# Loading the next seven-product chunk ahead of plain weight loads in a one-core decoder layer

## The chip, the cores and the metric

The kernel runs on one core of a Trainium2 chip. The metric is the device time of one execution in microseconds (us). The core's engines are TensorE (PE: matmuls; PEld is its weight load), VectorE (DVE), ScalarE (ACT), GpSimd (POOL) and SyncE (SP); each works through its own list of instructions in order. SP issues nearly all weight loads from memory; POOL issues loads and stores that add to what is there.

## The reference

One layer on 256 tokens of width 2048, in float32: a half-step gated feed-forward network (FFN) and a layer norm, then a mixer of two branches (attention over keys that an indexer selects, and a gated linear recurrence) and a layer norm, then a second FFN and a layer norm.

```python
def swiglu(h, w_in, w_out):
    a, b = jnp.split(h @ w_in, 2, axis=-1)
    return (jax.nn.silu(a) * b) @ w_out
...
h = layer_norm(DN_ALPHA * h + 0.5 * swiglu(h, ffn1_w_in[l], ffn1_w_out[l]), ln1_g[l], ln1_b[l])
q, k, v, qi, ki, wi, rx, rg, gates = split_cols(h @ w_in[l])
...
merged = g_attn * (y_attn @ w_attn_branch[l]) + g_rnn * (y_rnn @ w_rnn_branch[l])
h = layer_norm(DN_ALPHA * h + merged @ w_out[l], ln2_g[l], ln2_b[l])
h = layer_norm(DN_ALPHA * h + 0.5 * swiglu(h, ffn2_w_in[l], ffn2_w_out[l]), ln3_g[l], ln3_b[l])
```

The FFN's inner width is 5632. All weights are read once, so the kernel streams them through on-chip buffers while TensorE multiplies.

## The kernel before

Each float32 product is made of three matmuls on operands that are split into a high part and a rest: `wh` (made by ACT, line 268) and `wl` (made by DVE, line 269) of a weight, `xh` and `xl` of an activation; lines 727 to 729 are the three. So every weight passes a load (SP), a copy on ACT and a subtraction on DVE before PE can use it.

The weights are a list of pieces. A plain piece has 128x1024 elements (512 KB) and lands in a tile `raw`, of which there are 4. A chunk has 128x2048 elements (1 MB) and lands in a tile `rf`; it stands for four pieces in a row (`p1q3`, `p2`, `q5p7`, `q4p6`), since it is multiplied by a scheme of seven products in place of eight. For that DVE makes sums of the chunk's quarters first: `ws` (line 228) and two sums back into `rf` (lines 232 and 235). `rf` has 2 buffers; in the two FFNs a third one (tag `r3`) takes every third chunk. Chunks take these buffers in turn, so a chunk's buffer is free once the last split of the chunk three before it (two before it, where there are two buffers) is done on DVE.

`Weights.unit` hands PE its weights one after the other. Each time a new piece begins (`cur`), it runs `far_to` (pieces of f1o and f2o that are marked far: loaded early, split on ACT alone into `wd` by lines 180 and 183, with the rest made by POOL's adding load, line 181), then `load_to`, which issues loads up to 8 pieces ahead of `cur` in the order of the list (line 214; line 173 for far ones), and `split_to`, which splits up to 4 ahead.

The order of the instructions on PE, SP and POOL is that of the program. On ACT and DVE a scheduler sets it when the kernel is built, from its own estimate of when each instruction's inputs are there; on the chip that order is fixed, and an instruction that waits holds up all behind it on its engine.

The FFN runs in 22 blocks of 256 inner columns, each with four column groups of the first weight matrix (f1a, f2a). Blocks 6 to 21 of each FFN take all four as chunks: a block is three plain pieces of the second matrix (f1o, f2o: the `o` fills of blocks before it), two chunks, one more plain piece, two chunks. Two of the four plain pieces of a block are mostly far ones. Their finished sums leave as `yd` (ACT, line 1154), which POOL adds to memory (`ya`, line 1155).

Of the kernel before, what the change touches and what calls it, by code (L numbers as in the profile page):

```python
# [8 lines left out]
F32 = mybir.dt.float32  # L9
# [6 lines left out]
P = 128  # L16
# [41 lines left out]
RAWF_BUFS = 2  # L58
# [2 lines left out]
AHEAD = 4  # L61
EARLY = 12
LOADS = 4
FORMS = ("p1q3", "p2", "q5p7", "q4p6")
PIECE = 1024
FAST = (0, 1, 2, 3)
# [4 lines left out]
def block_plan(chunks, fills, lead=2, n=4, late=True):  # L71
# [3 lines left out]
    plain = [("c", k) for q in range(n) if q not in chunks for k in (4 * q, 4 * q + 2)]  # L75
    forms = [(f, q) for q in chunks for f in FORMS]
    rest = ["o"] * fills
# [58 lines left out]
class Weights:  # L136
# [8 lines left out]
    def __init__(self, nc, pool, pieces, on_piece):  # L145
        self.nc, self.pool, self.on_piece = nc, pool, on_piece
        self.fast_pool = self.third = None
        self.chunks = 0
        self.wide = None
        self.pieces = pieces  # L150
        self.raw = {}
        self.sums = {}
        self.hl = {}
        self.loaded = 0
        self.split = 0
        self.cur = -1
        self.limit = None
        self.cap = len(pieces)
        self.off = 0
        self.far = []  # L160
        self.apart = ()
        self.far_raw = {}
        self.far_loaded = self.far_split = 0

    def far_to(self, i):


        nc = self.nc
        while self.far_loaded < len(self.far) and self.far[self.far_loaded] <= i + LOADS:
            k = self.far[self.far_loaded]  # L170
# [24 lines left out]
    def load_to(self, i, between=None):  # L195
        nc = self.nc
        while self.loaded <= min(i, len(self.pieces) - 1):
            ap, form = self.pieces[self.loaded]
            k = self.key(self.loaded)
            if k not in self.raw and self.loaded not in self.far:  # L200
                n = ap.shape[1]
                if form:
                    self.chunks += 1
                    if self.third and self.chunks % 3 == 0:
                        t = self.third.tile([P, 2 * PIECE], F32, name=f"rf{self.loaded}", tag="r3", bufs=1)
                    else:
                        t = self.fast_pool.tile([P, 2 * PIECE], F32, name=f"rf{self.loaded}", tag="rf", bufs=RAWF_BUFS)
                else:
                    t = self.pool.tile([P, PIECE], F32, name=f"raw{self.loaded}", tag="raw", bufs=RAW_BUFS)
                self.raw[k] = t  # L210
                if between:
                    between(self.loaded)
                if self.loaded:
                    nc.sync.dma_start(t[:, :n], ap)
                else:
                    nc.sync.dma_start(t[:, :n // 2], ap[:, :n // 2])
                    nc.sync.dma_start(t[:, n // 2:n], ap[:, n // 2:])
            self.loaded += 1

    def operand(self, k, form):  # L220


        v = self.nc.vector
        b = self.raw[k].rearrange("p (r j c) -> p j r c", r=2, j=4)
        if form == "p1q3":
            t = self.fast_pool.tile([P, PIECE], F32, name=f"ws{self.split}", tag="ws", bufs=WS_BUFS)
            t = self.sums[k] = t.rearrange("p (f r c) -> p f r c", f=2, r=2)
            v.tensor_tensor(t, b[:, 0:4:3], b[:, 1:2].to_broadcast([P, 2, 2, 256]), op=OP.add)  # L228
            return b[:, 0:4:3]
        t = self.sums[k]  # L230
        if form == "p2":
            v.tensor_tensor(b[:, 1], t[:, 1], b[:, 0], op=OP.add)  # L232
            return b[:, 2:3]
        if form == "q5p7":
            v.tensor_tensor(b[:, 0], b[:, 1], b[:, 2], op=OP.add)  # L235
            return t
        del self.sums[k]
        return b[:, 0:2]

    def split_to(self, i, step=PIECE):  # L240
        nc = self.nc
        while self.split <= min(i, len(self.pieces) - 1):
# [27 lines left out]
            self.hl[self.split] = (h, l)  # L270
            if form in (None, FORMS[-1]):
                del self.raw[k]
            self.split += 1

    def unit(self, n):
        if self.cur < 0 or self.off == self.size(self.cur):
            self.hl.pop(self.cur, None)
            self.cur += 1
            self.off = 0
            self.far_to(self.cur + EARLY)  # L280
            self.load_to(self.cur + AHEAD + LOADS)
            self.split_to(self.limit or min(self.cur + AHEAD, self.cap))
            self.on_piece()
        h, l = self.hl[self.cur]
        o = self.off
        self.off += n
        assert self.off <= self.size(self.cur)
        if self.cur in self.apart or self.cur in self.far:
            return h[o // 512], l[o // 512]
        return h[:, o:o + n], l[:, o:o + n]  # L290
# [1379 lines left out]
```

## Time and profile before

| | |
|---|---|
| time, median of 3 runs | 2363.15 us (2363.1 to 2363.26) |
| the profiled execution's own time | 2361.44 us |
| its span, first to last instruction | 2359.6 us |
| PE busy | 2343.0 us (99%) |
| DVE busy | 2202.7 us (93%) |
| ACT busy | 1564.7 us (66%) |
| chunk loads of the FFNs (f1a, f2a) | 75 and 75, 1 MB each |
| read from memory | 507.10 MB |

Busy times of different engines overlap. A matmul's end is modelled, so a PE that is busy all the time can still be held up a little by each operand; the starts of its matmuls tell. Idle time of DVE, ACT and SP costs only what reaches PE.

### The profile page before, as it was taken

What the parts mean: (1) busy time and instruction counts of PE and PEld (TensorE: products, weight loads), DVE (VectorE), ACT (ScalarE), POOL (GpSimd) and SP (SyncE); (2) the same over time, 40 slices, a digit from 0 to 9 for tenths busy, and PEclk for the clock granted to TensorE, in tenths of its full rate; (3) what the DMA queues carried; (4) which work ended last, traced back from release to release, by engine and by line L of the source; (5) the groups of instructions that cost most, each with busy time, mean ns of one, the idle gap of its engine ahead of it and who ended that gap; (6) DMA issues with size and microseconds to landing.
All of it is one profiled execution on the core that took longest, in us unless ns stands there. A gap on an engine that the chain in (4) does not pass through costs nothing.

```text
span 2359.6 us, 40531 instructions
## 1 busy us (share of the span) xinstructions
PE 2343.0 (99%) x15430; PEld 2120.5 (90%) x15430; DVE 2202.7 (93%) x3197; ACT 1564.7 (66%) x2271; POOL 269.4 (11%) x376
## 2 busy tenths in 40 slices
PE   9999999999999999999999999999999999999998
PEld 7899999999988999888899998888889999999997
DVE  7999999999999999879887778998999999999997
ACT  7677777777656656556557785555767777777763
POOL 1111111111110000000100001100111111111111
PEclk9999999999999999999999999999999999999999
DMA  9888898888866555554665658755788888888876
GB/s 333 251 240 242 248 267 243 254 247 258 245 209 228 191 188 200 181 185 143 246 237 187 201 175 305 257 192 175 240 271 238 254 253 247 242 263 258 247 224 209
DMA packets 141667, 546.98 MB, mean 232 GB/s; under 512 B 16640, under 2 KB 17280, under 8 KB 117024
## 3 DMA queue, kind: packets, MB, share of 16 engines
q1 hardware_dynamic: 99792, 453.03, 54.8%
q0 software_dynamic: 41680, 91.36, 18.8%
q8 instruction: 121, 1.98, 0.3%
q14 instruction: 74, 0.61, 0.1%
HBM read 507.10 MB, written 37.22 MB: 231 GB/s over the span
## 4 chain that ended last, share of the span: by engine, by line
PE 86%; DVE 7%; issue 3%; DMA 2%; ACT 1%; POOL 0%; SPq 0%; POOLq 0%; ACTq 0%; DVEq 0%
PE mm L727 18%; PE mm L728 18%; PE mm L729 18%; PE bp L728 7%; PE bp L729 7%; PE bp L727 7%; DVE wl L269 4%; PE mm L1363 3%; PE mm L1364 3%; PE mm L1365 3%; DVE ws L228 1%; PE bp L1131 1%; DVE rf L232 1%; DVE rf L235 0%; ACT wh L268 0%
## 5 line engine op out<-in xcount | busy, mean ns | idle before, releaser
L268 ACT ACTIVATE wh<-rf 128x1024 fp32r<-128x1024 f32 x573 | 512.3, 913 | 236.6 <-DVE rf L235 123.1
L269 DVE TENSOR_TENSOR wl<-rf,wh 128x1024 fp32r<-128x1024 f32 x573 | 592.8, 1040 | 11.6 <-ACT wh L268 7.8
L268 ACT ACTIVATE wh<-raw 128x1024 fp32r<-128x1024 f32 (+3 forms) x402 | 409.8, 1038 | 205.4 <-PE mm L729 99.8
L269 DVE TENSOR_TENSOR wl<-raw,wh 128x1024 fp32r<-128x1024 f32 (+3 forms) x402 | 472.9, 1193 | 71.6 <-ACT wh L268 69.7
L728 PE MATMUL bp<-wl,sh 128*128 128x256 f32 x1146 | 322.5, 281 | 0.8 <-DVE wl L269 0.8
L727 PE MATMUL bp<-wh,sh 128*128 128x256 f32 x1146 | 320.5, 280 | 0.0
L729 PE MATMUL bp<-wh,sl 128*128 128x256 f32 x1146 | 320.2, 279 | 0.0
L727 PE MATMUL mm<-wh,hs 128*128 128x512 f32 (+1 forms) x800 | 276.1, 345 | 0.8 <-DVE z L1119 0.5
L729 PE MATMUL mm<-wh,hs 128*128 128x512 f32 (+1 forms) x800 | 270.1, 338 | 1.3 <-DVE hs L863 1.3
L728 PE MATMUL mm<-wl,hs 128*128 128x512 f32 (+1 forms) x800 | 269.7, 337 | 0.0
L268 ACT ACTIVATE wh<-ws 128x1024 fp32r<-128x1024 f32 x191 | 202.1, 1058 | 92.5 <-DVE ws L228 58.3
L228 DVE TENSOR_TENSOR ws<-rf 128x1024 f32<-128x1024 f32 x191 | 232.7, 1218 | 11.4 <-DMA rf<-wA 3.1
L269 DVE TENSOR_TENSOR wl<-ws,wh 128x1024 fp32r<-128x1024 f32 x191 | 232.4, 1217 | 3.0 <-ACT wh L268 3.0
L728 PEld LDWEIGHTS bp<-wl,sh 128*128 128x128 f32 x1146 | 215.4, 188 | 5.3 <-DVE wl L269 1.6
L727 PEld LDWEIGHTS bp<-wh,sh 128*128 128x128 f32 x1146 | 215.4, 188 | 1.5
L729 PEld LDWEIGHTS bp<-wh,sl 128*128 128x128 f32 x1146 | 215.4, 188 | 0.0
L1363 PE MATMUL mm<-hs,wh 128*128 128x256 f32 x640 | 180.3, 282 | 0.0
L1364 PE MATMUL mm<-hs,wh 128*128 128x256 f32 x640 | 179.8, 281 | 0.0
L1365 PE MATMUL mm<-hs,wl 128*128 128x256 f32 x640 | 179.8, 281 | 0.0
L729 PEld LDWEIGHTS mm<-wh,hs 128*128 128x128 f32 x800 | 150.2, 188 | 20.7 <-DVE hs L863 2.1
L727 PEld LDWEIGHTS mm<-wh,hs 128*128 128x128 f32 x800 | 150.3, 188 | 19.4 <-issue 2.2
L728 PEld LDWEIGHTS mm<-wl,hs 128*128 128x128 f32 x800 | 150.4, 188 | 16.1
(358 smaller groups left out, 5903.4 us busy)
## 6 DMA issues: line engine op xcount, KB each, us to landing
rf<-f1a SPq DMA_DIRECT2D x75, 1024.0 KB, 7.8
rf<-f2a SPq DMA_DIRECT2D x75, 1024.0 KB, 7.7
raw<-f1o SPq DMA_DIRECT2D x88, 512.0 KB, 6.6
raw<-f2o SPq DMA_DIRECT2D x88, 512.0 KB, 6.7
raw<-wB SPq DMA_DIRECT2D x80, 512.0 KB, 4.8
raw<-wG SPq DMA_DIRECT2D x54, 512.0 KB, 4.4
ya<-yd POOLq DMA_DIRECT2D x80, 256.0 KB, 7.8
rf<-wA SPq DMA_DIRECT2D x20, 1024.0 KB, 5.1
```

Of the source, the lines that this page charges most:

```text
L228: v.tensor_tensor(t, b[:, 0:4:3], b[:, 1:2].to_broadcast([P, 2, 2, 256]), op=OP.add)
L232: v.tensor_tensor(b[:, 1], t[:, 1], b[:, 0], op=OP.add)
L268: nc.scalar.activation(hp, src, AF.Copy)
L269: self.last = nc.vector.tensor_tensor(lp, src, hp, op=OP.subtract)
L727: T.matmul(ps, xh, w[0], start=start, stop=False)
L728: T.matmul(ps, xh, w[1], start=False, stop=False)
L729: T.matmul(ps, xl, w[0], start=False, stop=stop)
L1131: T.transpose(ps[:, k * S + t * P:k * S + (t + 1) * P], z[:, t * 512 + k * P:t * 512 + (k + 1) * P], ident)
L1363: T.matmul(ps[:, :S], w[0], x[:, 0], start=first, stop=False)
L1364: T.matmul(ps[:, :S], w[0], x[:, 1], start=False, stop=False)
L1365: T.matmul(ps[:, :S], w[1], x[:, 0], start=False, stop=last)
```

## The change

A new method `load_chunk` runs after `load_to` at each new piece. It looks up to 4 pieces past the last one loaded for a chunk whose load has not been issued. If that chunk's turn is not the third buffer's, none has been loaded early already, and fewer than 2 chunks stand unsplit before it, the chunk's load is issued at once, in front of the plain loads between. `load_to` then passes over it. Buffers, sizes and computation stay as they are.

```diff
--- before.py
+++ after.py
@@ -61,6 +61,7 @@
 AHEAD = 4
 EARLY = 12
 LOADS = 4
+CHUNK_LOADS = 4
 FORMS = ("p1q3", "p2", "q5p7", "q4p6")
 PIECE = 1024
 FAST = (0, 1, 2, 3)
@@ -152,6 +153,7 @@
         self.sums = {}
         self.hl = {}
         self.loaded = 0
+        self.early = set()
         self.split = 0
         self.cur = -1
         self.limit = None
@@ -197,6 +199,7 @@
         while self.loaded <= min(i, len(self.pieces) - 1):
             ap, form = self.pieces[self.loaded]
             k = self.key(self.loaded)
+            self.early.discard(k)
             if k not in self.raw and self.loaded not in self.far:
                 n = ap.shape[1]
                 if form:
@@ -216,6 +219,25 @@
                     nc.sync.dma_start(t[:, :n // 2], ap[:, :n // 2])
                     nc.sync.dma_start(t[:, n // 2:n], ap[:, n // 2:])
             self.loaded += 1
+
+    def load_chunk(self, end):
+
+
+        for i in range(self.loaded, min(end, len(self.pieces))):
+            ap, form = self.pieces[i]
+            k = self.key(i)
+            if not form or k in self.raw or i in self.far:
+                continue
+            if self.third and (self.chunks + 1) % 3 == 0 or self.early:
+                return
+            busy = {self.key(j) for j in range(self.split, i) if self.pieces[j][1]}
+            if len(busy) >= RAWF_BUFS:
+                return
+            self.chunks += 1
+            self.early.add(k)
+            t = self.raw[k] = self.fast_pool.tile([P, 2 * PIECE], F32, name=f"rf{i}", tag="rf", bufs=RAWF_BUFS)
+            self.nc.sync.dma_start(t, ap)
+            return
 
     def operand(self, k, form):
 
@@ -279,6 +301,7 @@
             self.off = 0
             self.far_to(self.cur + EARLY)
             self.load_to(self.cur + AHEAD + LOADS)
+            self.load_chunk(self.loaded + CHUNK_LOADS)
             self.split_to(self.limit or min(self.cur + AHEAD, self.cap))
             self.on_piece()
         h, l = self.hl[self.cur]
```

PE's and POOL's lists keep their order. SP's, ACT's and DVE's change. In 10 blocks of the first FFN and 11 of the second the load of the next block's first chunk moves ahead of two plain loads, one of them far; in the blocks between, whose next chunk is the third buffer's, nothing moves on SP. Elsewhere 47 more chunk loads move ahead of 1 to 3 loads (one near the start, ahead of 9).

SP in the middle of the first FFN, before; the number after the name is the piece. Chunk 274 is a block's fourth; the next block begins with plain 278, far 279 and plain 280, then come its chunks 281 and 285 and its far piece 289:

```order
L214 DMA rf274_5329<-f1a 128x2048
L214 DMA raw278_5409<-f1o 128x1024
L214 DMA raw280_5440<-f1o 128x1024
L173 DMA raw289_5459<-f1o 128x1024
L214 DMA rf281_5461<-f1a 128x2048
L214 DMA rf285_5527<-f1a 128x2048
```

and with the change:

```order
L217 DMA rf274_5329<-f1a 128x2048
L217 DMA raw278_5409<-f1o 128x1024
L239 DMA rf281_5411<-f1a 128x2048
L217 DMA raw280_5442<-f1o 128x1024
L175 DMA raw289_5461<-f1o 128x1024
L239 DMA rf285_5479<-f1a 128x2048
```

The chunk 281 now stands before plain 280 and far 289, which come after it.

ACT in the same block, from the third split of the block's third chunk (272) to the fourth of its fourth (277), before:

```order
L268 ACTIVATE wh272_5370<-ws270_5333 128x1024
L180 ACTIVATE wd352_5519<-raw289_5459 128x512
L180 ACTIVATE wd353_5520<-raw289_5459 128x512
L183 ACTIVATE wd350_5517<-raw289_5459 128x512
L268 ACTIVATE wh273_5387<-rf270_5258 128x1024
L1154 ACTIVATE yd348_5403<-mm335_5184 128x512
L1154 ACTIVATE yd349_5406<-mm336_5185 128x512
L268 ACTIVATE wh274_5411<-rf274_5329 128x1024
L268 ACTIVATE wh275_5429<-rf274_5329 128x512
L268 ACTIVATE wh276_5442<-ws274_5413 128x1024
L183 ACTIVATE wd351_5518<-raw289_5459 128x512
L268 ACTIVATE wh277_5463<-rf274_5329 128x1024
```

and with the change:

```order
L290 ACTIVATE wh272_5370<-ws270_5333 128x1024
L290 ACTIVATE wh273_5387<-rf270_5240 128x1024
L1177 ACTIVATE yd348_5403<-mm335_5184 128x512
L1177 ACTIVATE yd349_5406<-mm336_5185 128x512
L290 ACTIVATE wh274_5413<-rf274_5329 128x1024
L290 ACTIVATE wh275_5431<-rf274_5329 128x512
L290 ACTIVATE wh276_5444<-ws274_5415 128x1024
L182 ACTIVATE wd352_5521<-raw289_5461 128x512
L182 ACTIVATE wd353_5522<-raw289_5461 128x512
L185 ACTIVATE wd350_5519<-raw289_5461 128x512
L185 ACTIVATE wd351_5520<-raw289_5461 128x512
L290 ACTIVATE wh277_5463<-rf274_5329 128x1024
```

The three copies of far piece 289 that stood ahead of split 273 have moved behind split 276; all four now stand right ahead of split 277.

DVE from the third split of that fourth chunk on, before:

```order
L269 TENSOR_TENSOR wl276_5443<-ws274_5413,wh276_5442 128x1024
L269 TENSOR_TENSOR wl277_5464<-rf274_5329,wh277_5463 128x1024
L269 TENSOR_TENSOR wl278_5480<-raw278_5409,wh278_5479 128x1024
L269 TENSOR_TENSOR wl280_5502<-raw280_5440,wh280_5501 128x1024
L228 TENSOR_TENSOR ws281_5531<-rf281_5461 128x1024
```

and with the change:

```order
L291 TENSOR_TENSOR wl276_5445<-ws274_5415,wh276_5444 128x1024
L250 TENSOR_TENSOR ws281_5531<-rf281_5411 128x1024
L291 TENSOR_TENSOR wl277_5464<-rf274_5329,wh277_5463 128x1024
L291 TENSOR_TENSOR wl278_5482<-raw278_5409,wh278_5481 128x1024
L291 TENSOR_TENSOR wl280_5504<-raw280_5442,wh280_5503 128x1024
```

The sum `ws` of chunk 281 stood behind the two plain splits and now stands ahead of split 277.

## Rows read from the trace of the kernel before

**Rows 1.** The page's first lines: span; busy us of each engine, its share, instructions.

```profile
span 2359.6 us, 40531 instructions
PE 2343.0 (99%) x15430; PEld 2120.5 (90%) x15430; DVE 2202.7 (93%) x3197; ACT 1564.7 (66%) x2271; POOL 269.4 (11%) x376
```

**Rows 2.** Waits of PE: us in total, times, longest.

```profile
PE mm L727 <- ACT wh L268: 5.4, 1, 5.4
...
PE bp L728 <- DVE wl L269: 0.8, 3, 0.3
```

**Rows 3.** Windows of one block per FFN: busy us and instructions by engine, PEclk, DMA.

```profile
439.10:470.50 31.40, 31.40 (x222) 29.15 (x221) 31.29 (x38) 22.81 (x33) 5.33 (x6) 1.00 0.86 254
...
2112.50:2143.90 31.40, 31.40 (x221) 29.18 (x220) 31.30 (x38) 22.84 (x33) 5.30 (x6) 1.00 0.87 255
```

**Rows 4.** Timeline of DVE, one block: start, us, instruction.

```profile
457.19 1.22 DVE L269 TENSOR_TENSOR wl<-rf,wh 128x1024 fp32r<-128x1024 f32 x1
...
469.21 1.22 DVE L269 TENSOR_TENSOR wl<-ws,wh 128x1024 fp32r<-128x1024 f32 x1
470.50 1.23 DVE L269 TENSOR_TENSOR wl<-rf,wh 128x1024 fp32r<-128x1024 f32 x1
...
473.91 1.22 DVE L228 TENSOR_TENSOR ws<-rf 128x1024 f32<-128x1024 f32 x1
```

**Rows 5.** Timeline of PE at the same block's end.

```profile
470.48 0.39 PE L728 MATMUL bp<-wl,sh 128*128 128x256 f32 x1
...
472.00 0.28 PE L728 MATMUL mm<-wl,xs 128*128 128x256 f32 x1
```

**Rows 6.** Timeline of SP, same block.

```profile
451.76 0.33 SPq L214 DMA_DIRECT2D rf<-f1a  x1
452.18 0.86 SPq L214 DMA_DIRECT2D raw<-f1o  x2
453.09 0.73 SPq L173 DMA_DIRECT2D raw<-f1o  x1
458.44 13.64 SPq L214 DMA_DIRECT2D rf<-f1a  x3
```

**Rows 7.** Timeline of ACT, same block.

```profile
461.63 1.14 ACT L180 ACTIVATE wd<-raw 128x512 fp32r<-128x512 f32 x2
462.67 0.62 ACT L183 ACTIVATE wd<-raw 128x512 fp32r<-128x512 f32 x1
...
466.57 1.05 ACT L268 ACTIVATE wh<-ws 128x1024 fp32r<-128x1024 f32 x1
467.52 0.63 ACT L183 ACTIVATE wd<-raw 128x512 fp32r<-128x512 f32 x1
469.41 1.06 ACT L268 ACTIVATE wh<-rf 128x1024 fp32r<-128x1024 f32 x1 [1.26 <-DVE rf L235]
```

**Rows 8.** DMA issues from 451 to 458 us: size, median us to landing.

```profile
raw<-f1o SPq DMA_DIRECT2D x3, 512.0 KB, 6.5
rf<-f1a SPq DMA_DIRECT2D x1, 1024.0 KB, 4.9
```

**Rows 9.** DMA queues from 463.5 to 468.5 us: packets, MB, share of 16 engines.

```profile
q0 software_dynamic: 397, 0.74, 92.5%
q1 hardware_dynamic: 35, 0.20, 11.8%
```

**Rows 10.** DMA queues and issues from 409 to 412 us.

```profile
q1 hardware_dynamic: 18, 0.04, 5.2%
...
rf<-f1a SPq DMA_DIRECT2D x1, 1024.0 KB, 8.1
```

**Rows 11.** Timeline of ACT, another moved block.

```profile
398.87 1.15 ACT L180 ACTIVATE wd<-raw 128x512 fp32r<-128x512 f32 x2 [0.29 <-DMA raw<-f1o]
```

**Rows 12.** Timeline of SP in the mixer's first part.

```profile
855.80 0.33 SPq L214 DMA_DIRECT2D rf<-wA  x1
```

**Rows 13.** Timeline of ACT, same stretch.

```profile
860.93 2.95 ACT L268 ACTIVATE wh<-raw 128x1024 fp32r<-128x1024 f32 x3
```

## The prediction

> **What bounds the kernel now.** I read the page's busy times first, then PE's waits, then the windows of single blocks, then the timelines of DVE, SP and ACT at one block's end. The page gives PE 2343.0 of 2359.6 us, but also DVE 2202.7 [rows 1]. PE's waits are almost nothing: the longest is 5.4 us at the start, and line 728's waits for DVE's `wl` come to 0.8 us [rows 2]. So there is next to nothing to win on PE. The windows show that there is much to lose: in a block of four chunks DVE is busy 31.29 of 31.40 us, in the first FFN as in the second [rows 3]. DVE runs level with PE there. A wait that DVE takes on in such a block makes the block longer, since it has no idle time in which to work it off.
>
> The timelines show how tight the end of a block is. `wl` of the fourth chunk's third split starts at 469.21 and ends at 470.43; the one of its fourth split starts at 470.50 [rows 4]. PE's matmuls on them start at 470.48 and 472.00 [rows 5]: the first has no slack, the second 472.00 - 471.73 = 0.27 us. ACT, on the other hand, has 8.6 us idle in a block (31.40 - 22.81) [rows 3], and it waits for DVE before the copy at 469.41 [rows 7]. I call the moment at which chunk 281's buffer comes free T0: DVE's last split on the old chunk runs from 457.19 to 458.41 [rows 4], and SP issues the load at 458.44 [rows 6].
>
> **The chunk load itself.** It gains nothing in these blocks. SP stood waiting for that buffer already, with all loads in front of it issued by 453.8 [rows 6]; the buffer comes free when DVE says so, before and after. What changes is who stands behind it: plain 280 and far 289, issued before T0 until now (452.6 and 453.09), are issued after T0, about 0.4 and 0.9 us behind the chunk. Nothing else queues on SP that is due soon.
>
> **Plain 280** is issued 6.3 us later. ACT copies it two copies behind the one at 469.41 [rows 7], so not before 471, and it lands ahead of 289 (below). No cost.
>
> **Far 289** is the term. ACT now makes its four copies at once, behind the copy that starts at 466.57 and ends at 467.62 [rows 7], which is T0 + 9.2. If it has not landed by then, ACT waits, and behind it stand the copy for the fourth split of the fourth chunk, and with that DVE's `wl` and PE.
>
> When does it land? Alone on the queue, the same amount (one chunk and two plain loads) takes 7.4 us: the chunk issued at 451.76 took 4.9, and the middle one of the three plain loads, issued at 452.61, landed 6.5 later, at 459.1 [rows 6, 8]. That is the lower end: T0 + 7.4, 1.8 us early. But 5 us after T0 POOL's adding transfers run. From 463.5 to 468.5 they hold 92.5% of the DMA engines, and SP's queue gets 11.8% [rows 9]. A second stretch says that this is not for want of work on SP's side: from 409 to 412 a chunk's load was out that took 8.1 us in place of 4.9, and its queue held 5.2% [rows 8, 10]. So the load of 289 runs free for 5.1 us (458.44 to 463.5) and has 2.3 of its 7.4 us left; in the next 5 us it gets about a tenth, some 0.55; the last 1.75 us follow after 468.5. It lands at 470.2, T0 + 11.8. The upper end is a queue that is shut out wholly for those 5 us: T0 + 12.4. I take 11.8, which is what the row of that very stretch gives.
>
> The Trainium skill says otherwise: "DMA: Bandwidth & Descriptors", section on queues, rings and completion order, has each DMA engine take the queues in turn, a packet of each. With half the engines' time SP's queue would do the 2.3 us in 4.6, and 289 would land at T0 + 9.7; that costs nothing, by rival 1. The rows above have SP's queue at 5 to 12%, not at half, so the trace does not agree.
>
> Then the rest of the chain. Four copies: two take 1.14 us in a row, so one step is 0.52 [rows 7], four are 2.1; the copy for the fourth split is 1.06, and DVE follows 0.03 later. `wl` of the fourth split starts at 470.2 + 2.1 + 1.06 + 0.03 = 473.4 in place of 470.50: 2.9 us later. In that wait DVE makes the next chunk's `ws`, which stood behind (473.91 to 475.05 in step, 1.14) [rows 4], so DVE loses 2.9 - 1.14 = 1.76 us a block. At the lower end ACT does not wait; `ws` then comes first at 470.43 and `wl` follows at 471.57, 1.07 later with 1.14 done: 0.07 won. At the upper end it is 2.36 lost. What is late next is PE's line 728 on that `wl`, and the whole next block with it.
>
> That ACT stops for a far load this trace has already: at 398.87 it waited 0.29 us for one to land [rows 11], with the load still issued 5 us ahead of the chunk.
>
> **How often.** 21 blocks move this way. I leave out the first in each FFN, behind a block with fewer chunks, where DVE is not yet level with PE; that leaves 19: 19 x 1.76 = 33.4 us (-1.3 to +45).
>
> **The other blocks** (every third) keep SP's order. ACT and DVE have theirs but for a few rows; nothing is counted.
>
> **Elsewhere** 47 chunk loads move ahead of one to three plain ones. Where they gain, there is no wait of PE to take away [rows 2]. Where they block, the tightest place is in the mixer's first part: three plain loads now follow the chunk load of 855.80 [rows 12] and land behind it: the chunk takes 4.9 us and each plain one (7.4 - 4.9) / 2 = 1.2 more, so the first lands at 861.9, where ACT used it at 860.93 [rows 13]. That is one microsecond late on ACT, and PE uses what ACT makes one or two pieces later. By the order I count some five places of this kind. I take 2 us for all (-3, all of PE's waits but that at the start gone, to +8, more than 1 us at each).
>
> **The sum** is made against the profiled execution's own 2361.44: + 33.4 + 2 = 2396.8. The median of the runs shown stands 1.7 above it, so the forecast is 2398.5, rounded 2398 (+1.5%).
>
> **The rivals.**
>
> 1. SP's queue shares the engines better than the rows say. If far 289 lands by T0 + 9.9, `wl` can follow `ws` at 471.57 (471.57 - 3.19 of copies = 468.4). Then ACT's four copies cost nothing, DVE's small gaps close by 0.07 us in 19 blocks, and the elsewhere term remains: 2363.15 - 1.3 + 2, some 2364. No change. For it: the DMA engines are not full over a block (0.86) [rows 3], SP's queue had little to carry in a part of the stretch of rows 9, since the chunk of 458.44 lands within it, and far 289's new place in the queue has an empty queue ahead of it. Against it: SP's queue at 11.8% and 5.2% while POOL's transfers ran [rows 9, 10]. The Trainium skill's round robin ("DMA: Bandwidth & Descriptors", the same section) is a rule by which it would go this way.
>
> 2. Faster. The three far copies ahead of split 273 are gone, so split 274's copy comes earlier, `ws` fills the gap before the fourth split, and DVE lets PE run without the short stalls at the block's end. PE's start at 470.48 with 0.39 in place of 0.28 us [rows 5] is such a stall, some 0.1 us, and there are two or three a block: 0.28 us x 19 = 5.3 us at most, and perhaps 3 elsewhere: 2355. It decides if 289 lands before T0 + 9.2, where ACT is ready for it. Against it: DVE's 31.29 us of work are the same, so no more than 0.11 a block is there on its side [rows 3].
>
> 3. Worse than forecast. SP's queue is shut out wholly, and PE, late by then, hands its sums to `yd` later, so that the adding transfers end 0.4 us later: 2.76 a block, in all 21, is 58, and 8 elsewhere: 2429.
>
> 4. The change does not act, since SP waits for the buffer anyhow: true of the chunk load, not of those behind it. It is rival 1 in time.
>
> **How the numbers follow.** A measurement of this kernel can tell about 0.2%, 4.7 us. The forecast and all that ends slower than 2367.9 (rival 3 in it, 0.06) get 0.78; rival 1 and with it 4 get 0.15, all within 2358.4 to 2367.9; rival 2 gets 0.07. The range goes from 2362, which takes in most of rival 1, to 2422, past the upper ends together (2363.15 + 45 + 8 = 2416), toward rival 3; what is left out is rival 2 and most of rival 3. The forecast's own range is 2375 (289 at T0 + 10.7) to 2422.
>
> **What would show it.** In the blocks that moved, ACT waits 2 to 3 us for a far load's landing ahead of `wd`, DVE is idle for some 1.8 us before `wl` of the fourth split, PE waits for `wl` on line 728 about 20 times, 2 to 3 us each, and the block takes 33.2 us, while the third blocks keep 31.4. The DMA page shows the far loads at 11 us from issue in place of 7. If the far loads land within 9 us of issue, or ACT's wait is there and the block is still 31.4 long, the reasoning is wrong at that step. If the moved blocks are at 31.4 and the time moves anyway, it came from the mixer.

## The result and the profile after

The changed kernel took 2380.61 us (median of 6 runs, 2379.58 to 2381.36), the kernel before 2363.12 beside it: a ratio of 1.0076, 95% interval 1.0066 to 1.0086. The change makes the kernel 17.5 us slower. The forecast was 2398, so the direction held, and the forecast loss of 35 us was twice the measured one.

The page's first lines of the changed kernel [rows 1 are those of before]:

```profile
span 2377.7 us, 40464 instructions
...
PE 2348.2 (99%) x15430; PEld 2120.5 (89%) x15430; DVE 2206.2 (93%) x3197; ACT 1567.0 (66%) x2271; POOL 268.9 (11%) x376
```

The work is the same (DVE 3.5 us more, PE 5.2) and the span is 18.1 longer. The waits say where. First ACT's, then DVE's, then PE's of the changed kernel (us in total, times, longest):

```profile
ACT wd L182 <- DMA raw<-f2o: 18.1, 12, 3.7
ACT wd L182 <- DMA raw<-f1o: 15.5, 11, 3.4
```

```profile
DVE wl L291 <- ACT wh L290: 99.9, 115, 2.3
```

```profile
PE mm L751 <- DVE wl L291: 10.6, 18, 0.9
...
PE bp L751 <- DVE wl L291: 2.4, 4, 0.9
```

The kernel before had these in place of the first three, nothing in place of PE's `mm`, and 0.8 for its `bp` [rows 2]:

```profile
DVE wl L269 <- ACT wh L268: 80.5, 99, 2.3
...
ACT wd L180 <- DMA raw<-f2o: 1.4, 2, 0.9
...
ACT wd L180 <- DMA raw<-f1o: 0.3, 1, 0.3
```

Nearly all of the 33.6 us in which ACT stands before `wd` are new; DVE waits 19 us longer for ACT's `wh`; PE waits 22 times for `wl`.

Matching PE's matmuls one by one between two traces gives how late each kernel is at a moment of the kernel before (us, in the profiled execution of each; e1 to e10 are the experiments below by number, and e5 and e6 a pair):

```
before  after    e1    e2    e8    e7   e10    e3  |  e5     e6
 206.1   0.60  1.69  0.42  0.95  0.63  1.51  1.26  | 0.84   1.06
 231.1   4.26  1.73  0.91  1.18  6.65  1.73  1.49  | 1.12   1.10
 447.2   6.47  1.31  2.08  1.41  8.38  3.19 10.30  | 1.36   0.70
 608.1   9.55  1.29  2.50  1.59  8.89  3.70 10.50  | 1.56   0.75
1692.2   9.32  1.30  1.33  0.10  9.74  2.92 11.23  | 0.82   0.57
1892.0  13.36  1.64  4.31  2.24 13.06  3.07 11.61  | 0.70  -0.30
1905.0  14.92  1.64  5.09  2.82 14.63  3.89 12.28  | 2.27  -0.30
2334.2  18.21  1.70  9.02  6.52 15.66  9.83 20.54  | 2.09  -0.45
```

The loss is in the two FFNs, 9.0 and 8.9 us; between 608 and 1692, where the mixer runs, there is none. Windows of three blocks in a row of the changed kernel (busy us and instructions of PE, PEld, DVE, ACT, POOL; PE's clock; DMA share; GB/s), against 31.40 a block before [rows 3]:

```profile
445.64:476.86 31.22, 31.22 (x223) 29.10 (x222) 31.11 (x39) 20.69 (x30) 4.00 (x5) 1.00 0.80 245
476.86:509.85 32.99, 31.75 (x223) 29.22 (x221) 31.68 (x39) 24.45 (x35) 6.61 (x8) 1.00 0.80 244
509.85:541.48 31.63, 31.48 (x222) 29.16 (x221) 31.52 (x39) 23.85 (x34) 5.33 (x6) 1.00 0.87 251
```

Only the middle one is long: DVE has 31.68 us of work in 32.99 and is idle for 1.31, in place of 0.11. What happens where the first window passes into the second, in the timelines, SP first, then ACT, then DVE (answering to [rows 6], [rows 7] and [rows 4]):

```profile
464.28 0.33 SPq L239 DMA_DIRECT2D rf<-f1a  x1
464.66 0.42 SPq L217 DMA_DIRECT2D raw<-f1o  x1
465.13 0.85 SPq L175 DMA_DIRECT2D raw<-f1o  x1
```

```profile
472.35 1.06 ACT L290 ACTIVATE wh<-ws 128x1024 fp32r<-128x1024 f32 x1
475.46 1.16 ACT L182 ACTIVATE wd<-raw 128x512 fp32r<-128x512 f32 x2 [2.05 <-DMA raw<-f1o]
476.52 1.14 ACT L185 ACTIVATE wd<-raw 128x512 fp32r<-128x512 f32 x2
477.56 1.04 ACT L290 ACTIVATE wh<-rf 128x1024 fp32r<-128x1024 f32 x1
```

```profile
475.09 1.22 DVE L291 TENSOR_TENSOR wl<-ws,wh 128x1024 fp32r<-128x1024 f32 x1
476.34 1.23 DVE L250 TENSOR_TENSOR ws<-rf 128x1024 f32<-128x1024 f32 x1
478.64 1.23 DVE L291 TENSOR_TENSOR wl<-rf,wh 128x1024 fp32r<-128x1024 f32 x1 [1.07 <-ACT wh L290]
```

This is the predicted chain, link by link. T0 is 464.28; the far load lands at 475.38, T0 + 11.1; ACT stands 2.05 us for it, makes four copies in 2.1 and the `wh` copy; DVE does `ws` in the meantime and is then idle for 1.07. By the prediction's sum a landing at T0 + 11.1 costs 11.1 - 11.8 + 1.76 = 1.06.

### The profile page after: what moved, and what is told of

Same layout as the page of the kernel before. It is cut to its first block, busy times and chain, and to the rows that moved or that the text cites. A ratio compares the mean times of both kernels' runs of the same rounds, so it can differ in the third digit from the quotient of the medians.

```text
span 2377.7 us, 40464 instructions
## 1 busy us (share of the span) xinstructions
PE 2348.2 (99%) x15430; PEld 2120.5 (89%) x15430; DVE 2206.2 (93%) x3197; ACT 1567.0 (66%) x2271; POOL 268.9 (11%) x376
## 3 DMA queue, kind: packets, MB, share of 16 engines
q0 software_dynamic: 41680, 91.36, 18.1%
## 4 chain that ended last, share of the span: by engine, by line
PE 81%; DVE 11%; issue 3%; ACT 2%; DMA 2%; SPq 0%; POOL 0%; POOLq 0%; ACTq 0%; DVEq 0%
PE mm L751 17%; PE mm L750 16%; PE mm L752 16%; PE bp L752 6%; PE bp L751 6%; PE bp L750 6%; DVE wl L291 6%; PE mm L1388 3%; PE mm L1386 3%; PE mm L1387 3%; ACT wh L290 2%; DVE ws L250 2%; DVE rf L257 1%; DVE rf L254 1%; PE bp L1154 1%
## 5 line engine op out<-in xcount | busy, mean ns | idle before, releaser
L752 PEld LDWEIGHTS mm<-wh,hs 128*128 128x128 f32 x800 | 150.2, 188 | 19.6 <-DVE hs L944 1.3
```

Of the source, the lines that this page charges most:

```text
L752: T.matmul(ps, xl, w[0], start=False, stop=stop)
```

## The experiments

The theory: the loss comes from ACT's in-order wait for far loads that stand behind the chunk in SP's queue. Rival A: the other order on DVE (`ws` ahead of `wl`) costs by itself. Rival B: the chunk's earlier place, with its traffic, costs by itself.

**1. The far load first, then the early chunk** (in `load_chunk` of the changed kernel):

```diff
             self.early.add(k)
+            while self.far_loaded < len(self.far) and self.far[self.far_loaded] <= i + 8:
+                f = self.far[self.far_loaded]
+                t = self.far_raw[f] = self.pool.tile([P, PIECE], F32, name=f"raw{f}", tag="raw", bufs=RAW_BUFS)
+                self.nc.sync.dma_start(t, self.pieces[f][0])
+                self.far_loaded += 1
```

> The changed kernel, but where the chunk is loaded early, the far load that would come due within the next few pieces is issued first, then the chunk. Theory (the far load behind the chunk reaches ScalarE's in-order wd copy too late, and the copies and the wl subtraction behind it come late on VectorE, which has no slack): the far load lands some 2 us sooner than in the changed kernel, ScalarE's waits at wd for f1o and f2o fall from 33.6 us together to under 3 us, and the time is 2363 us, give or take 3. Rival A (the new order of ws and wl on VectorE that the early load brings is itself what costs): the order still differs from the kernel before, so the time stays at 2376 to 2381 us. Rival B (having the chunk on the queues earlier slows the other transfers): also 2376 to 2381 us.

2363.19 us, ratio 1.0004 (0.9996 to 1.0013): nothing is left of the loss. SP in the block of the rows above, then ACT's waits:

```profile
453.92 0.42 SPq L239 DMA_DIRECT2D raw<-f1o  x1
459.74 0.33 SPq L244 DMA_DIRECT2D rf<-f1a  x1
460.12 0.42 SPq L217 DMA_DIRECT2D raw<-f1o  x1
```

```profile
ACT wd L182 <- DMA raw<-f2o: 3.0, 1, 3.0
...
ACT wd L182 <- DMA raw<-f1o: 0.3, 1, 0.3
```

The far load (453.92) is issued before the chunk's buffer comes free, the chunk still ahead of the plain load. The early chunk as such costs nothing, so rival B falls. Rival A is not settled by this run: its order on DVE is neither that of the changed kernel nor that of the kernel before.

**2. The kernel before, with only the far load put behind the chunk** (in `unit`):

```diff
-            self.far_to(self.cur + EARLY)
-            self.load_to(self.cur + AHEAD + LOADS)
+            i = self.cur + AHEAD + LOADS
+            if i < len(self.pieces) and self.pieces[i][1] == FORMS[0] and self.third and (self.chunks + 1) % 3:
+                self.load_to(i)
+            self.far_to(self.cur + EARLY)
+            self.load_to(i)
```

> The kernel before, with one thing done to it: in the blocks that the change touches, the chunk's load is issued just ahead of the far load instead of just behind it; it does not pass any plain load, and the step of the loop in which it is issued stays. Theory: the far load then waits behind a megabyte on SP's queue as in the changed kernel, ScalarE waits at wd for 20 to 35 us in all, and the time is 2375 to 2383 us (most of the 17.5 us of the change). Rivals A and B (the new order on VectorE, or the chunk's earlier place as such): 2363 us, give or take 3, since neither the chunk's step nor the plain loads move.

2369.26 us, ratio 1.0030 (1.0019 to 1.0041): 6.9 us, above the rivals' value and below the expected one. What I had not counted is that in the changed kernel a plain load stands between chunk and far load (464.66 above), and here it does not. The far loads land at T0 + 7.3 to 9.2, and ACT waits 11.9 us at `wd` in place of 33.6 (in one of the 21 blocks the far load landed at 11.9):

```profile
ACT wd L180 <- DMA raw<-f2o: 7.4, 5, 3.9
...
ACT wd L180 <- DMA raw<-f1o: 4.5, 5, 1.7
```

Not all of the 6.9 us is the far load's. In seven blocks of the second FFN this kernel loses 0.36 to 0.40 us each, some 2.7 us together, without a wait of ACT at `wd`. DVE's order is another there, though the edit moves no more than one load a block, and its `wl` waits for a `wh` copy that ACT makes behind `yd`. Experiment 8 shows the same; it is rival A, in small:

```profile
2049.60 1.23 DVE L269 TENSOR_TENSOR wl<-rf,wh 128x1024 fp32r<-128x1024 f32 x1 [0.41 <-ACT wh L268]
```

**3. The far pieces' copies three pieces later**, all loads as in the changed kernel:

```diff
+FAR_LATER = 3
...
-        while self.far_split < len(self.far) and self.far[self.far_split] <= i:
+        while self.far_split < len(self.far) and self.far[self.far_split] <= i - FAR_LATER:
```

> The changed kernel, all loads in its order, but the copies of a far piece (wd and the rest of its split) are put three pieces later in the program. Theory: the far load is just as late (about 10 us after the chunk's buffer comes free), but ScalarE reaches the copy only after it has landed, so its waits at wd fall under 3 us and the time is 2363 us, give or take 4. Rival A (the order of ws and wl) and rival B (the early chunk's traffic): loads and VectorE's work are those of the changed kernel, so 2376 to 2383 us.

2382.37 us, ratio 1.0085 (1.0073 to 1.0097): a miss. ACT's waits at `wd` for f1o and f2o are gone, but not only for the expected reason: with POOL's adding transfers later, the far loads of 20 of the 21 blocks land sooner, at T0 + 7.2 to 9.0. The adding transfers are issued behind ACT's copies and moved with them. PE now waits for them:

```profile
PE mm L752 <- DMA wd<-f1o: 7.4, 6, 2.3
PE mm L752 <- DMA wd<-f2o: 6.1, 5, 3.2
```

With the two longest of these waits TensorE's granted clock also fell to 0.50 for 3.4 us (from 357.7 and from 1944.9), which it does in no other kernel there. One wait has taken another's place, so the run tells nothing between the theories; experiments 7 and 10 try shorter delays.

**4. The change outside the FFNs only:**

```diff
-            if self.third and (self.chunks + 1) % 3 == 0 or self.early:
+            if self.third or self.early:
```

> The change only outside the two FFN parts, where no far loads are issued; in the FFNs the chunks are loaded as in the kernel before. Theory: without a far load behind a chunk nothing is late, 2363 us, give or take 2. A rival by which early chunk loads as such cost: the mixer holds about a third of the moved loads, so 2366 to 2370 us; one by which they gain there: under 2361 us.

2362.90 us, ratio 1.0001 (0.9992 to 1.0009). The moved loads outside the FFNs, which have no far load behind them, neither cost nor gain.

**5 and 6. The changed kernel and the kernel before with POOL's adding transfers cut to 32 columns:**

```diff
-                nc.gpsimd.dma_start(l[c], ap[:, c * 512:(c + 1) * 512], accum_op=OP.add)
+                nc.gpsimd.dma_start(l[c][:, :32], ap[:, c * 512:c * 512 + 32], accum_op=OP.add)
...
-                    G.dma_start(acc[t][nb], u, accum_op=OP.add)
+                    G.dma_start(acc[t][nb][:, :32], u[:, :32], accum_op=OP.add)
```

> The changed kernel with POOL's adding transfers in the FFNs (the rest of the far pieces' split and the partial outputs) cut from 512 to 32 columns each; the other 480 columns of those sums are left out. All engines' instructions and all of SP's loads stay. Theory: with no big transfers beside it, SP's queue brings chunk, plain load and far load one after the other in about 5 + 1 + 1 us, the far load lands 7 to 7.5 us after the chunk's buffer comes free, which is before ScalarE's slot at 9.2, and this kernel and its counterpart without the change agree within 3 us. Rivals A and B (order on VectorE; the chunk's early place as such): still 13 to 18 us between the two.

> The kernel before with the same cut of POOL's adding transfers to 32 columns (the other columns of those sums left out): the measure for the changed kernel with that cut. VectorE and TensorE do the same work, so 2355 to 2364 us by every theory; only the distance between the two counts.

2363.16 and 2360.43 us, ratios 1.0001 (0.9992 to 1.0010) and 0.9991 (0.9982 to 1.0000): 2.7 us between them in place of 17.5. The queues of experiment 5, five microseconds after T0 + 5 (packets, MB, share of 16 engines), and then two lines of its DMA issues (count, size, median us to landing):

```profile
q1 hardware_dynamic: 289, 1.35, 80.4%
q0 software_dynamic: 297, 0.03, 12.1%
```

```profile
rf<-f1a SPq DMA_DIRECT2D x75, 1024.0 KB, 4.9
...
raw<-f1o SPq DMA_DIRECT2D x88, 512.0 KB, 5.8
```

The order on every engine is that of the changed kernel. With SP's queue nearly alone on the engines the far loads land at T0 + 7.5 to 8.9, and ACT's waits at `wd` fall from 33.6 to 4.2 us. Contention with POOL's adding transfers is what makes the far loads late, and 14.8 of the 17.5 us go with it. At most the other 2.7 are left to rival A, the order. Some of that is there: between 1892 and 1905 experiment 5 falls back by 1.6 us in the table, without a wait of ACT at `wd`, and the changed kernel, which has the same order, by the same 1.6.

**7. The copies one piece later, and 10. two pieces later** (`FAR_LATER` 1 and 2 in place of 3):

> The changed kernel with the copies of a far piece put one piece later instead of three: three were too many, since POOL's adding transfers then landed after TensorE wanted wd (13.5 us of waits that no other kernel has). One piece is about 1.6 us, so ScalarE reaches wd at about 10.8 after the chunk's buffer comes free, and the far loads land at 9.8 to 11.1. Theory: waits at wd for f1o and f2o fall from 33.6 to under 8 us, TensorE waits for no adding transfer, 2364 to 2371 us. Rivals A and B: 2378 to 2383 us, as the loads and VectorE's order are those of the changed kernel.

> The changed kernel with the copies of a far piece two pieces later. One piece later left 19.6 us of ScalarE's 33.6 us of waits at wd and gave 2374 us; three pieces later left 3 us of them but made TensorE wait 13.5 us for POOL's adding transfers. Theory: two pieces (about 3.1 us) put ScalarE's copy at about 12.3 after the chunk's buffer comes free, behind nearly every far load, so under 8 us of waits at wd; the adding transfers, which were 1.2 us late on average with three, are late by under 3 us in all; 2364 to 2371 us. Rivals A and B: 2378 to 2383 us, since the loads and VectorE's order are still those of the changed kernel.

2374.22 us, ratio 1.0052 (1.0040 to 1.0065), and 2370.82, ratio 1.0035 (1.0021 to 1.0049). ACT's waits of the two kernels, in that order:

```profile
ACT wd L183 <- DMA raw<-f2o: 10.8, 7, 4.1
...
ACT wd L183 <- DMA raw<-f1o: 8.8, 6, 3.2
```

```profile
ACT wd L183 <- DMA raw<-f2o: 7.7, 7, 2.9
...
ACT wd L183 <- DMA raw<-f1o: 2.6, 3, 1.6
```

With 33.6, 19.6 and 10.3 us of waits at `wd` the loss to the kernel before in the same runs is 17.5, 11.8 and 9.5 us. (Experiment 3 had left none of them, not the 3 us that the second text names.) The direction is the theory's; one piece later was short of its numbers by 3 us, two pieces later met the time and missed the waits. As in experiment 3 the far loads did not stay where they were: they land at 9.6 on average in both, in place of 10.3. In the table 6.0 of the loss of one piece later comes in one block, between 206 and 231. The changed kernel has the same block, and loses 3.7 there. The ACT and DVE of the changed kernel:

```profile
215.76 0.63 ACT L290 ACTIVATE wh<-rf 128x512 fp32r<-128x512 f32 x1
219.83 0.63 ACT L182 ACTIVATE wd<-raw 128x512 fp32r<-128x512 f32 x1 [3.44 <-DMA raw<-f1o]
220.37 1.04 ACT L290 ACTIVATE wh<-ws 128x1024 fp32r<-128x1024 f32 x1
```

```profile
221.44 1.23 DVE L291 TENSOR_TENSOR wl<-ws,wh 128x1024 fp32r<-128x1024 f32 x1 [2.15 <-ACT wh L290]
```

Here one `wd` copy stands ahead of the `wh` copy for the third split, not only ahead of the fourth. The same late load then holds up a `wl` that DVE wants sooner, and no `ws` fills the gap. One piece later has the same order and much the same waits there (3.21 and 1.92 us). The other 2.4 us are not the theory's: in that kernel's profiled execution, its slowest of five, TensorE's granted clock then stood at 0.50, the lower of its two levels (1.2 in place of 2.4 GHz), and in the changed kernel it did not. That kernel and then the changed one (columns as in the windows above):

```profile
223.90:230.70 6.80, 6.17 (x23) 5.20 (x22) 6.80 (x9) 4.59 (x6) 0.00 (x0) 0.50 0.95 282
223.90:230.70 6.80, 5.97 (x34) 5.01 (x33) 6.77 (x10) 4.60 (x7) 0.00 (x0) 1.00 0.96 283
```

In the 4.9 us before, PE was busy for 3.10 us in the one and 2.94 in the other, so the rows do not tell why it fell in one alone. Two pieces later has such a stretch too, 3.4 us from 2249.4. So these two runs bear out the direction, but their sizes hold other things too.

**8. The far load second: chunk, far load, plain load** (the lines of experiment 1, put behind the chunk's own load):

```diff
             self.nc.sync.dma_start(t, ap)
+            while self.far_loaded < len(self.far) and self.far[self.far_loaded] <= i + 8:
...
             return
```

> The changed kernel with one swap in SP's queue: behind the early chunk comes the far load and then the plain load, instead of the plain load and then the far load. Theory with the measured share: half a megabyte less stands ahead of the far load, so it lands 2 to 2.6 us sooner, at 7.4 to 8.3 after the chunk's buffer comes free, and the time is 2363 to 2370 us (the kernel before with the far load right behind the chunk gave 2369). Rival A (order on VectorE) and rival B (early chunk as such): 2378 to 2382 us.

2369.21 us, ratio 1.0029 (1.0019 to 1.0040). Half a megabyte less in front of the far load moves its landing to T0 + 6.8 to 8.9 (in 20 of 21 blocks; 11.0 in one) and takes back 11 of the 17.5 us, as expected. But a landing at 7.3 on average in these 20 should have cost nothing, and 6.7 us are still lost, nearly all in the second FFN. ACT there, then DVE:

```profile
2043.55 1.05 ACT L295 ACTIVATE wh<-ws 128x1024 fp32r<-128x1024 f32 x1
2045.66 0.60 ACT L1182 ACTIVATE yd<-mm 128x512 f32<-128x512 f32 x1 [1.06 <-PE mm L757]
2046.15 1.05 ACT L295 ACTIVATE wh<-rf 128x1024 fp32r<-128x1024 f32 x1
```

```profile
2047.24 1.23 DVE L296 TENSOR_TENSOR wl<-rf,wh 128x1024 fp32r<-128x1024 f32 x1 [0.43 <-ACT wh L295]
2048.38 1.22 DVE L255 TENSOR_TENSOR ws<-rf 128x1024 f32<-128x1024 f32 x1
```

That is rival A at work, in small: DVE's `wl` now stands ahead of its `ws` in this place, and waits 0.43 us for a copy that ACT makes behind `yd`. In the kernel before and in experiment 1 `ws` stood ahead of it and covered that wait. Seven blocks of this kernel lose 0.38 to 0.41 us, 2.7 together. Most of the rest comes at three places in the second FFN where ACT still waits for a far load (2.9, 3.0 and 1.1 us, at 1722, 1796 and 2145). Where the order was put otherwise, as in experiment 5, the cost is lower; which order comes out is the scheduler's choice in each kernel.

No kernel here beats the kernel before by more than its measurement tells. Experiments 1 and 4 equal it.

## Why the prediction was half right

**PE has nothing to gain, DVE decides in the FFN blocks:** right. In three blocks DVE has 94.31 us of work in 95.84, and each wait of it shows in the block's length.

**The chunk load gains nothing, plain 280 costs nothing:** right. With the far load out of the way the change is worth 0 (experiment 1).

**ACT's wait for the far load goes through `wh` and DVE's `wl` to PE, less the `ws` made in the wait:** right, to 0.01 us of DVE's idle time in the block shown, where the real landing is put in. The block as PE sees it lost 1.6, some 0.5 more than DVE's wait: by the windows DVE is idle for 1.20 us more than in a block before and busy for 0.39 more. Where that comes from stays open.

**"In the next 5 us it gets about a tenth ... It lands at 470.2, T0 + 11.8":** this step failed. In 17 moved blocks where the three issues stand close together, the far load landed at T0 + 9.5 to 11.3, 10.2 on average (in the other four up to 11.7); it begins to cost at 10.04 (11.8 less the 1.76 that it was to cost). In 16 of the 21 blocks ACT's list has the predicted order. There eight landings before 10.04 cost -0.1 to 0.4 us each by the matched matmuls, and six at 10.5 to 11.1 cost 0.9 to 1.8; the other two came at 10.1. The queues of the changed kernel in the five microseconds from T0 + 5 (469.4 to 474.4; packets, MB, share of 16 engines):

```profile
q1 hardware_dynamic: 244, 0.97, 56.2%
q0 software_dynamic: 270, 0.49, 53.4%
```

SP's queue (q1) holds half, not a tenth, and it does so all along: 53.2 to POOL's 54.4% in the first 2.5 us, 59.2 to 52.3% in the rest. The tenth of [rows 9] is made of two things. Until the chunk of 458.44 landed at 465.92, the queue had little left to carry (0.15 MB from 463.5 to 466). But the next chunk was issued at 466.38, and until 468.5 it moved next to nothing. [Rows 10] are the same: a chunk issued at 408.94. So is the kernel before one stretch further, where the same chunk runs almost alone from 469 to 471.5, and the chunk and the far load issued at 471.75 and 472.13 get next to nothing until 474:

```profile
q1 hardware_dynamic: 96, 0.79, 89.0%
q0 software_dynamic: 28, 0.05, 13.2%
...
q0 software_dynamic: 220, 0.42, 93.3%
q1 hardware_dynamic: 28, 0.10, 12.2%
```

So the low shares were real, but they belong to loads that were issued while POOL's transfers ran. The far load of the changed kernel was issued ahead of them: it went out at 465.13, and in all of 463.5 to 468.5 no packet of POOL's queue ran. That is the step: the prediction gave it the share of loads in the other position. That the position makes the difference is read from these cases; no run varied it alone. Rival 1 named a part of this (the queue had little to carry, and far 289 has an empty queue ahead of it), and I set it aside for [rows 10]. The Trainium skill's rule ("DMA: Bandwidth & Descriptors", section on queues, rings and completion order: each engine takes the queues in turn) agrees with the changed kernel's stretch, 56 to 53%. Whether the 5 to 12% of the kernel before go against it cannot be told here, since the rows do not show when an issued load reaches the engines. The prediction's estimate by that rule, T0 + 9.7, was 0.5 off the mean; mine was 1.6 off.

**19 x 1.76 = 33.4:** the term measured 17.9 in the two FFNs (9.0 + 8.9). It is not a like loss in each block. In five of the 21 ACT's list has a `wd` copy ahead of the `wh` copy for the third split, so that the late load hits a split sooner, which the sum did not have: they lost 0 to 3.7 us, two of them 1.2 and 1.0 at a landing of 9.8. And 1.6 of the 17.9 are the order's, not the load's (experiment 5). With the 21 landings as they were, the prediction's own sum would have given 7.4 us in all; the same blocks lost 19 by the matched matmuls, and 1 was won back elsewhere. So that the time lies within the forecast's own range is luck in part: a landing taken too late made up for orders that the sum left out.

**Mixer +2:** within what can be told it was 0 (experiment 4, -1.9 to +2.1 us by its interval, and the table from 608 to 1692).

**The rivals.** Rival 1 had the right rate and the wrong time: its threshold of T0 + 9.9 was about right too, but the blocks lie on both sides of it, and it took them all for early. Rival 2 (faster), rival 3 (shut out) and rival 4 (no effect) are out: PE's line 751 waits more, not less; the latest far load of all 21 came at 11.7, not at 12.4; and ACT's waits appear.

**Signs named ahead.** ACT's wait of 2 to 3 us was 2.05 in the block shown; DVE idle of 1.8 was 1.07; PE's 20 waits of 2 to 3 us for `wl` were 22 of 0.9 at most, 13.0 us in all of the 18.2 by which it ends later; the block of 33.2 is 32.99 in the rows above, and about every second moved block is a long one.

## What to carry to other kernels

A load moved ahead in an in-order queue is paid for by those it passes: look for the one whose consumer stands in an in-order engine ahead of something critical, and keep that load in front, as experiment 1 does for nothing. A queue's low share in a stretch is a rate under contention only if it had a transfer under way all through it, and here only for a load issued in the same position, while the other queue ran and not ahead of it; check issues and landings, and cut the stretch in halves, since an even mean can hide two one-sided parts. And a delay near a threshold needs the spread of the landings, not one landing times the number of blocks.

## What the runs showed of the hardware

With both queues at work, and SP's loads issued ahead of POOL's transfers, the engines' time was split about evenly in the changed kernel (56.2 and 53.4%), but SP's loads moved twice the bytes of POOL's adding transfers in it (0.97 to 0.49 MB). POOL's adding transfers cost a one-megabyte load of `f1a` 2.9 us in the median: 7.8 us to landing in the kernel before, 4.9 with them cut (experiments 5 and 6).

A load issued while they run moved next to nothing for a microsecond or more. In the kernel before, with a chunk issued at 466.38, the queues from 466 to 468.5 us were:

```profile
q0 software_dynamic: 197, 0.35, 98.8%
q1 hardware_dynamic: 6, 0.05, 6.3%
```

[Rows 10] show the same right behind the issue of 408.94, and the rows from 471.5 to 474 above behind that of 471.75. Why a load waits there was not tried and stays open.
